# A decoder step on one core: the first loads are cut and spread over two queues, the squares wait for the first conversions, and the first products go to the convolution's banks

## The chip, the cores and the metric

The kernel runs on one core of a Trainium2 chip. It uses the core's five engines: TensorE (PE, matrix products, with PEld for its weight loads), VectorE (DVE), ScalarE (ACT), GpSimd (POOL) and SyncE (SP), which here only issues DMAs. The metric is the device time of one execution in microseconds (us); the median of several runs is compared.

## The reference

One decoder layer is applied to 256 prompt tokens and 8 x 4 sample tokens, 288 columns in all. Cut to what matters here:

```python
h = rmsnorm(x, norm1_g)                              # 2048 channels
proj = einsum("btd,de->bte", h, w_in) + b_in         # 2048 -> 3072
a, gate, z = split(proj, 1024)
u = a * sigmoid(gate)                                # convolution group
c = silu(layernorm(depthwise_causal_conv(concat(hist_conv, u), conv_w, conv_b)))   # 31 taps
d = multiscale_pool(concat(hist_pool, z))            # windows 2, 4, 8, 16
p = einsum("btgc,gce->btge", d, pool_w) * pool_scale
x = x + concat(c, p) @ w_out
h2 = rmsnorm(x, norm2_g)
x = x + square(relu(h2 @ w_ff1)) @ w_ff2             # 2048 -> 8192 -> 2048
y = rmsnorm(x, norm_f)
```

The outputs are `y` for both groups and the last 30 columns of `u` and the last 15 of `z`.

## The kernel before

Channels lie on the 128 partitions and the 288 token columns on the free axis: `xT` holds 16 channel tiles of 288 columns. Weights come from memory in blocks of 1024 input channels by 256 output columns (1 MB, `load`, L146). `split` (L213) turns each block into two halves of four channel tiles, and each half into a high part `whi` (ScalarE, L225) and a low part `wlo`, the rest (VectorE or GpSimd, L228; `SHARE` says how many halves of each kind go to GpSimd). Inputs are split in the same way. `gemm` (L237) forms each result from three products per channel tile: high by high (L250), high weight by low input (L251), low weight by high input (L252).

The input projection is done in 12 groups, in the order of `SEQUENCE`: seven convolution groups, four pool groups, and the eighth convolution group. A convolution group gives 128 columns of `a` (m = 0) and their 128 gates (m = 1). Each group is 16 channel tiles x 2 halves x 3 = 96 products. The text calls the convolution groups blocks 0, 1, 2 and so on. Two blocks of weights belong to each group; the first two, `raw0` and `raw1`, are loaded in quarters, each behind the matching two channel tiles of `xT` (L158, L159).

The norm is applied after the product. `hx` (L271, L272) is `x` times the gain only; the reciprocal root of the mean square is found beside the products: `squares` (L299) squares `xT` on ScalarE (L304) and adds the squares on VectorE (L306), `rsqrt_sums` (L181) adds over the partitions with TensorE (the tile `pt`, L186) and forms the root through a short chain on VectorE and ScalarE to `dg` (L198), and `spread` (L201) brings it to all partitions with one more product (the tile `pr`, L204). ScalarE copies it to `rb` (L395). Before, the program asks for `pt` ahead of channel tile 10 of block 1 and for `pr` ahead of tile 14 of block 1.

`conv_pair` (L320) multiplies a convolution group's result by `rb` (L325), applies the gate (L326, L330), and then runs the 31 taps: the first on ScalarE (L337), 30 on VectorE (L340), the sample tokens on GpSimd and VectorE (L343, L345). The taps stand in a `later` block, which puts them behind all other work in priority. `pool_group` (L354) does the same for a pool group, with its running sums on GpSimd (L369); `dx` is its result split in two parts, `px` the product with `pool_w` (L417, L418).

Results of the products go to banks of PSUM: `acc` has two double banks (the tile `ac`), `cvp` two single banks (tag `cv`, used by the taps' running sum `pc`), `msp` two single banks for the small products.

The order of instructions on each engine isn't the program's. A planner reads the program with its dependencies, plays it through with a model of the costs, and lets each engine take the ready instruction of the highest priority; priority is the program's order, and `later` puts a block behind. On the chip each engine then runs its list in that order. Twelve products of `ones` with itself (L173) run at the start, ahead of the first weights.

Of the kernel before, what the change touches and what calls it, by code (L numbers as in the profile page):

```python
# [9 lines left out]
F32 = mybir.dt.float32  # L10
# [6 lines left out]
P = 128  # L17
# [55 lines left out]
for _k, _n in VEC:  # L73
    OFF[_k] = NV
    NV += _n
CWO = NV
# [4 lines left out]
def trunk_kernel(ctx: ExitStack, tc: tile.TileContext, io):  # L81
# [64 lines left out]
    def load(cuts=((0, 8),), x_cuts=()):  # L146

        raw = wraw.tile([P, 8, 256], F32, name=nm("wr"), tag="wr")
        src = io["w"][next(blocks)]
        for j, (k0, k1) in enumerate(cuts):  # L150
            if j < len(x_cuts):
                a, b = x_cuts[j]
                nc.sync.dma_start(xT[:, a:b, :], io["xT"][:, a:b, :])
            nc.sync.dma_start(raw[:, k0:k1, :], src[:, k0:k1, :])
        return raw

    nc.scalar.dma_start(vec[:, 0:CWO], io["vec"][:, 0:CWO])
# [14 lines left out]
    for j in range(12):  # L172
        nc.tensor.matmul(warm[:, 0:P], ones, ones, start=True, stop=True)  # L173
# [37 lines left out]
    turn = {"n": 0}  # L211

    def split(raw, share=0, cut=4):  # L213
# [3 lines left out]
        for h in range(2):  # L217
# [5 lines left out]
            for k in range(0, 4, cut):  # L223
                src = raw[:, 4 * h + k : 4 * h + k + cut, :]
                nc.scalar.copy(hi[:, k : k + cut, :], src)  # L225
                eng, step = (nc.gpsimd, 2) if slow else (nc.vector, cut)
                for j in range(k, k + cut, step):
                    eng.tensor_tensor(lo[:, j : j + step, :], raw[:, 4 * h + j : 4 * h + j + step, :], hi[:, j : j + step, :].bitcast(F32), op=ALU.subtract)  # L228
            parts.append((hi, lo))

# [45 lines left out]
    def weight_groups():  # L276

        yield [split(raw0, SHARE["first"], 2), split(raw1, SHARE["first"], 2)]
# [20 lines left out]
    def squares():  # L299
# [20 lines left out]
    def conv_pair(i, bk):  # L320
# [4 lines left out]
        nc.vector.tensor_tensor(ag, bk[:, :, :T], both(rb), op=ALU.mult)  # L325
# [28 lines left out]
    def pool_group(g):  # L354
# [236 lines left out]
```

## Time and profile before

| what | us |
|---|---|
| median of 3 runs | 1122.28 (1120.97 to 1122.3) |
| the profiled execution: its own time | 1121.02 |
| its span, first to last instruction | 1119.2 |
| TensorE busy in the span | 1095.0 (98%) |
| VectorE, ScalarE, GpSimd busy | 646.2, 470.1, 185.8 |
| mean granted clock of TensorE | 0.990 |

A row of a timeline gives the start in us from the span's start, the duration, the engine, the line of the kernel, the operation, what it writes and reads, and the shapes; in brackets stands the idle time of the engine just before and what ended it. Products overlap in TensorE's pipeline, so the step from start to start is what counts there; on ScalarE and VectorE too neighbours overlap a little. A row of stages gives, for a stretch of time, each engine's busy time and number of instructions, TensorE's granted clock, the share of the DMA engines' time that is used, and the rate in GB/s.

### The profile page before, as it was taken

How to read it: one execution, taken by the hardware profiler on the slowest of the kernel's cores; microseconds unless marked ns; L12 is line 12 of the kernel's file. 1: busy time of each engine (PE TensorE's matmuls, PEld its weight loads, DVE VectorE, ACT ScalarE, POOL GpSimd, SP SyncE). 2: the span in 40 equal slices, each digit the busy share in tenths (PEclk: the TensorE clock that was granted, in tenths of full speed). 3: DMA queues.
4: the chain of work that ended last, by engine and by line, in shares of the span. 5: the costliest groups of instructions: out<-in, count | busy, mean ns of one | idle time of the engine just before them, and what ended most of it. 6: DMA issues, size and time to landing. Idle time of an engine off the chain costs nothing.

```text
span 1119.2 us, 19178 instructions
## 1 busy us (share of the span) xinstructions
PE 1095.0 (98%) x8220; PEld 1090.7 (97%) x8220; DVE 646.2 (58%) x830; ACT 470.1 (42%) x578; POOL 185.8 (17%) x185
## 2 busy tenths in 40 slices
PE   9999988999999999999999999999999999999995
PEld 8999987999999999999999999999999999999995
DVE  7799999667654444444554444455444445554553
ACT  8444444465444433334443333444433334444441
POOL 1898996512100000000000000000000000000000
PEclk9999998999999999999999999999999999999997
DMA  9545456444444454544445444454544545445432
GB/s 344 186 154 185 151 132 201 154 176 161 160 168 162 161 179 153 179 159 164 175 154 182 153 168 171 155 184 152 172 167 160 180 151 177 162 159 180 152 112 85
DMA packets 31909, 187.00 MB, mean 167 GB/s; under 512 B 3408, under 2 KB 7760, under 8 KB 10448
## 3 DMA queue, kind: packets, MB, share of 16 engines
q1 hardware_dynamic: 31680, 185.73, 48.1%
q8 instruction: 64, 1.05, 0.4%
q14 instruction: 21, 0.17, 0.0%
q10 hardware_dynamic: 144, 0.05, 0.0%
HBM read 181.49 MB, written 4.28 MB: 166 GB/s over the span
## 4 chain that ended last, share of the span: by engine, by line
PE 93%; POOL 2%; DVE 2%; DMA 1%; ACT 1%; issue 1%; SPq 0%; DVEq 0%; ACTq 0%; POOLq 0%
PE ac L250 31%; PE ac L252 31%; PE ac L251 30%; POOL wlo L228 1%; POOL s L369 1%; DMA wr<-in_w 1%; PE pt L186 0%; DMA xT<-in_xT 0%; DVE xT L531 0%; ACT whi L225 0%; ACT hx L271 0%; PE pr L204 0%; DVE px L418 0%; DVE hx L272 0%; DVE pc L340 0%
## 5 line engine op out<-in xcount | busy, mean ns | idle before, releaser
L225 ACT CAST whi<-wr 128x1024 fp32r<-128x1024 f32 (+1 forms) x342 | 355.2, 1040 | 563.6 <-PE ac L251 531.9
L228 DVE TENSOR_TENSOR wlo<-wr,whi 128x1024 fp32r<-128x1024 f32 (+1 forms) x297 | 364.0, 1226 | 352.2 <-ACT whi L225 351.3
L250 PE MATMUL ac<-ax,whi 128*128 128x288 f32 x1024 | 303.4, 296 | 0.0
L250 PE MATMUL ac<-fx,whi 128*128 128x288 f32 x1024 | 303.1, 296 | 0.0
L252 PE MATMUL ac<-ax,wlo 128*128 128x288 f32 x1024 | 301.8, 295 | 0.0
L252 PE MATMUL ac<-fx,wlo 128*128 128x288 f32 x1024 | 301.8, 295 | 0.0
L251 PE MATMUL ac<-ax,whi 128*128 128x288 f32 x1024 | 298.5, 292 | 0.0
L251 PE MATMUL ac<-fx,whi 128*128 128x288 f32 x1024 | 298.5, 292 | 0.0
L251 PEld LDWEIGHTS ac<-ax,whi 128*128 128x128 f32 x1024 | 192.5, 188 | 0.1
L251 PEld LDWEIGHTS ac<-fx,whi 128*128 128x128 f32 x1024 | 192.5, 188 | 0.0
L250 PEld LDWEIGHTS ac<-ax,whi 128*128 128x128 f32 x1024 | 192.4, 188 | 0.1
L250 PEld LDWEIGHTS ac<-fx,whi 128*128 128x128 f32 x1024 | 192.4, 188 | 0.0
L252 PEld LDWEIGHTS ac<-ax,wlo 128*128 128x128 f32 x1024 | 191.5, 187 | 0.0
L252 PEld LDWEIGHTS ac<-fx,wlo 128*128 128x128 f32 x1024 | 191.5, 187 | 0.0
L228 POOL TENSOR_TENSOR wlo<-wr,whi 128x512 fp32r<-128x512 f32 x90 | 119.4, 1358 | 48.1 <-ACT whi L225 48.1
L252 PE MATMUL ac<-hx,wlo 128*128 128x288 f32 x384 | 114.8, 299 | 1.5 <-DVE wlo L228 1.3
L250 PE MATMUL ac<-hx,whi 128*128 128x288 f32 x384 | 114.8, 299 | 0.3 <-ACT whi L225 0.3
L251 PE MATMUL ac<-hx,whi 128*128 128x288 f32 x384 | 112.7, 294 | 0.0
L340 DVE SCALAR_TENSOR_TENSOR pc<-u_all,vec,pc 128x256 f32<-128x256 f32 x232 | 99.4, 480 | 1.2
L252 PEld LDWEIGHTS ac<-hx,wlo 128*128 128x128 f32 x384 | 72.6, 189 | 3.4 <-DVE wlo L228 2.5
L250 PEld LDWEIGHTS ac<-hx,whi 128*128 128x128 f32 x384 | 72.9, 190 | 0.6 <-ACT whi L225 0.5
L251 PEld LDWEIGHTS ac<-hx,whi 128*128 128x128 f32 x384 | 72.9, 190 | 0.1
(109 smaller groups left out, 828.4 us busy)
## 6 DMA issues: line engine op xcount, KB each, us to landing
wr<-in_w SPq DMA_DIRECT2D x167, 1024.0 KB, 4.9
xT<-in_xT SPq DMA_DIRECT2D x8, 288.0 KB, 5.7
wr<-in_w SPq DMA_DIRECT2D x8, 256.0 KB, 5.6
out_u_out<-u_all SPq DMA_DIRECT2D x1, 1208.0 KB, 8.9
out_yT<-xT SPq DMA_DIRECT2D x2, 576.0 KB, 2.9
u_all<-in_hist_c SPq DMA_DIRECT2D x8, 136.0 KB, 6.1
out_z_out<-z_all SPq DMA_DIRECT2D x1, 668.0 KB, 8.1
z_all<-in_hist_p SPq DMA_DIRECT2D x4, 152.0 KB, 5.6
```

What stands on the lines that cost most here:

```text
L225: nc.scalar.copy(hi[:, k : k + cut, :], src)
L228: eng.tensor_tensor(lo[:, j : j + step, :], raw[:, 4 * h + j : 4 * h + j + step, :], hi[:, j : j + step, :].bitcast(F32), op=ALU.subtract)
L250: nc.tensor.matmul(b, wh, xh, start=k == 0, stop=False)
L251: nc.tensor.matmul(b, wh, xl, start=False, stop=False)
L252: nc.tensor.matmul(b, wl, xh, start=False, stop=k == n - 1)
L340: nc.vector.scalar_tensor_tensor(out=dst, in0=up[:, w : w + SEQ], scalar=cwv[:, w : w + 1], in1=pc, op0=ALU.mult, op1=ALU.add)
L369: nc.gpsimd.tensor_tensor(s2[:, m, 2 * w - 1 :], s[:, m, 2 * w - 1 :], s[:, m, w - 1 : ZL - w], op=ALU.add)
```

## The change

It has five parts.

1. The first loads. Only the first 16 columns of `vec` (`norm1_g`, `NG` columns) are loaded ahead, on ScalarE's queue, followed on the same queue by channel tile 0 of the first weight block. SyncE's queue loads tile 0 and then tile 1 of `xT`, tile 1 of the weights, and then two tiles of `xT` and two of the weights in turn, as before. The other columns of `vec` come at the end of these loads. The conversions of the first weight block are cut to match: tiles 0, 1, 2 to 3, and so on.
2. Nine products of `ones` at the start in place of twelve.
3. `squares` begins with a copy on ScalarE of ten elements of the last `whi` tile of block 0 into the first column of the squares' scratch. Each square writes there too, so all eight follow the last conversion of block 0. In the program they stand behind the conversions of block 1, as before.
4. Block 0's products go to two single banks of `cvp` in place of a double bank of `acc`. The sums for the norm (`pt`) are asked for ahead of tile 15 of block 1, and `pr` and the copy to `rb` ahead of tile 3 of block 2; block 2's products stand ahead of `conv_pair(0)` in the program.
5. The multiply by `rb` is done for `a` and for the gates by two instructions of 288 columns each, in all eight convolution groups, in place of one of 576.

```diff
-    def load(cuts=((0, 8),), x_cuts=()):
+    def load():
...
-    nc.scalar.dma_start(vec[:, 0:CWO], io["vec"][:, 0:CWO])
-    raw0 = load(((0, 2), (2, 4), (4, 6), (6, 8)), ((0, 2), (2, 4), (4, 6), (6, 8)))
-    raw1 = load(((0, 2), (2, 4), (4, 6), (6, 8)), ((8, 10), (10, 12), (12, 14), (14, 16)))
-    nc.sync.dma_start(vec[:, CWO:NV], io["vec"][:, CWO:NV])
...
+    def piece(queue, what, a, b):
+        if what == "x":
+            queue.dma_start(xT[:, a:b, :], io["xT"][:, a:b, :])
+        else:
+            queue.dma_start((raw0, raw1)[a // 8][:, a % 8 : a % 8 + b - a, :], firsts[a // 8][:, a % 8 : a % 8 + b - a, :])
+
+    nc.scalar.dma_start(vec[:, 0:NG], io["vec"][:, 0:NG])
+    piece(nc.scalar, "w", 0, 1)
+    piece(nc.sync, "x", 0, 1)
+    piece(nc.sync, "x", 1, 2)
+    piece(nc.sync, "w", 1, 2)
+    for k in range(2, KT, 2):
+        piece(nc.sync, "x", k, k + 2)
+        piece(nc.sync, "w", k, k + 2)
+    nc.sync.dma_start(vec[:, NG:NV], io["vec"][:, NG:NV])
...
-    for j in range(12):
+    for j in range(9):
...
-    def split(raw, share=0, cut=4):
+    def split(raw, share=0, cuts=(0, 4, 4, 8)):
...
+            for a, b in zip(cuts, cuts[1:]):
+                if a // 4 == h and a < b:
+                    nc.scalar.copy(hi[:, a % 4 : a % 4 + b - a, :], raw[:, a:b, :])
+                    eng, step = (nc.gpsimd, 2) if slow else (nc.vector, b - a)
+                    for j in range(a, b, step):
+                        part = slice(j % 4, j % 4 + step)
+                        eng.tensor_tensor(lo[:, part, :], raw[:, j : j + step, :], f32(hi[:, part, :]), op=ALU.subtract)
             parts.append((hi, lo))
+        last_hi.append(hi)
...
-        yield [split(raw0, SHARE["first"], 2), split(raw1, SHARE["first"], 2)]
+        yield [split(raw0, SHARE["first"], (0, 1, 2, 4, 6, 8)), split(raw1, SHARE["first"], (0, 2, 4, 6, 8))]
...
-    def squares():
+    def squares(hi):
+
+        nc.scalar.copy(scratch[:, :, :, 0:1], f32(hi)[:, 3, 0:10].rearrange("p (n k t) -> p n k t", n=5, t=1))
...
-        bk = bank2()
-        gemm(each(bk), hx, **kw)
-        return bk
+        if i:
+            banks = each(bank2())
+        else:
+            banks = [cvp.tile([P, 512], F32, name=nm("ac"), tag="cv") for m in range(2)]
+        gemm(banks, hx, **kw)
+        return banks
...
-        nc.vector.tensor_tensor(ag, bk[:, :, :T], both(rb), op=ALU.mult)
+        for m in range(2):
+            nc.vector.tensor_tensor(ag[:, m, :], banks[m][:, :T], rb, op=ALU.mult)
...
+    last = last_hi[-1]
     first = conv_products(0)
-    squares()
+    squares(last)
     diag = []
-    second = conv_products(
-        1,
-        between={
-            10: lambda: diag.append(rsqrt_sums([t[:, m, :] for t in tot for m in range(2)], 1.0 / D, AF.Sigmoid)),
-            14: lambda: nc.scalar.copy(rb, spread(diag[0])[:, :T]),
-        },
-    )
+    second = conv_products(1, between={15: lambda: diag.append(rsqrt_sums([t[:, m, :] for t in tot for m in range(2)], 1.0 / D, AF.Sigmoid))})
+    third = conv_products(2, between={3: lambda: nc.scalar.copy(rb, spread(diag[0])[:, :T])})
     nc.gpsimd.memset(z_all[:, :, 0:PH], 0.0)
     conv_pair(0, first)
     conv_pair(1, second)
-    for kind, i in SEQUENCE[2:]:
+    conv_pair(2, third)
+    for kind, i in SEQUENCE[3:]:
```

More of the change, by code (lines that the diff above doesn't have):

```diff
@@ L208, in rsqrt_rows @@
         return spread(rsqrt_sums(*args))
-    turn = {"n": 0}
-    def split(raw, share=0, cut=4):
+    turn, last_hi = {"n": 0}, []
+    def split(raw, share=0, cuts=(0, 4, 4, 8)):
         parts = []
@@ L315, in conv_products, with conv_pair @@
         nc.sync.dma_start(u_all[:, i, UO:UL], io["hist_c"][:, i, :])
[L316 to L320 removed]
+        if i:
[4 more added lines that the diff above has]
+        return banks
+    def conv_pair(i, banks):
         up = u_all[:, i, 0:UO]
```

16 lines of the change are left out of this document (4 added, 12 removed).

## The prediction

> **What bounds the kernel now.** I read the page first, then the engines' busy time by stage, then the instructions of the first 40 us on each engine, the landings of the first loads, and last the three long waits of TensorE behind 160 us. Five stages (columns: stretch, length, then busy us and count of PE, PEld, DVE, ACT, POOL, then granted clock, DMA share, GB/s):
>
> ```profile
> 6.30:21.20 14.90, 13.52 (x91) 12.14 (x92) 14.84 (x28) 14.75 (x30) 0.00 (x0) 1.00 1.05 401
> 21.20:37.60 16.40, 16.40 (x132) 16.29 (x131) 7.24 (x13) 8.47 (x12) 10.85 (x9) 1.00 0.90 319
> 37.60:160.00 122.40, 122.24 (x921) 121.67 (x921) 121.74 (x244) 53.63 (x77) 115.85 (x104) 1.00 0.43 150
> 160.00:190.00 30.00, 21.02 (x121) 20.24 (x120) 28.77 (x56) 13.39 (x22) 20.31 (x18) 0.83 0.81 215
> 190.00:1100.00 910.00, 910.00 (x6894) 909.68 (x6893) 465.37 (x474) 375.03 (x433) 37.44 (x33) 1.00 0.47 162
> ```
>
> TensorE sets the end. Its steady step is 910 / 6894 = 0.132 us a product, so 96 of them, one channel block, are 12.67 us. Two places have idle steps: the head, up to 21.2, and 160 to 190 (121 products are 16 us of the 30). In the head ScalarE and VectorE are full (14.75 and 14.84 of 14.90) and so are the DMAs (share 1.05). From 37.6 to 160 TensorE, VectorE (121.74 of 122.40) and GpSimd (115.85) are all full. The change touches the head alone, but it moves the start of VectorE's full stretch too.
>
> The ledger of the head, from TensorE's timeline and VectorE's:
>
> ```profile
> 6.32 0.40 PE L250 MATMUL ac<-hx,whi 128*128 128x288 f32 x1 [0.27 <-ACT whi L225]
> ...
> 21.18 1.78 PE L186 MATMUL pt<-ones,z_all 128*96 128x1 f32 x20
> 22.82 0.38 PE L250 MATMUL ac<-hx,whi 128*128 128x288 f32 x1
> ...
> 35.33 0.65 PE L204 MATMUL pr<-dg,ones 96*128 96x288 f32 x2
> 37.61 0.76 DVE L325 TENSOR_TENSOR ag<-ac,rb 128x576 f32<-128x576 f32 x1 [0.40 <-PE ac L252]
> ```
>
> The second multiply by `rb` waits for the last product of block 1, so block 1 ends at 37.6. Backwards from there: 14.78 us from 22.82, less 0.5 for `pr`, hold 108 products, that is block 1 and the last two channel tiles of block 0. So block 0 ended at about 24.4. From 6.32 to 37.6 are 31.3 us; 192 products (25.3), `pt` (3 columns, 4 parts, 2 passes: 24, about 2.0) and `pr` (0.5) need 27.8. **3.5 us** are lost.
>
> Where: one pair of channel tiles on ScalarE, then on VectorE.
>
> ```profile
> 8.49 0.96 ACT L271 ACTIVATE hx<-xT,vec 128x288 fp32r<-128x288 f32 x2
> 9.36 0.67 ACT L304 ACTIVATE z_all<-xT 128x576 f32<-128x576 f32 x1
> 9.94 0.60 ACT L225 CAST whi<-wr 128x512 fp32r<-128x512 f32 x1
> 10.45 0.96 ACT L271 ACTIVATE hx<-xT,vec 128x288 fp32r<-128x288 f32 x2
> ...
> 9.28 0.94 DVE L272 SCALAR_TENSOR_TENSOR hx<-xT,vec,hx 128x288 fp32r<-128x288 f32 x2
> 10.13 0.75 DVE L306 TENSOR_TENSOR z_all<-z_all 128x576 f32<-128x576 f32 x1
> 10.80 0.69 DVE L228 TENSOR_TENSOR wlo<-wr,whi 128x512 fp32r<-128x512 f32 x1
> 11.40 0.94 DVE L272 SCALAR_TENSOR_TENSOR hx<-xT,vec,hx 128x288 fp32r<-128x288 f32 x2
> ```
>
> By starts a pair costs ScalarE 10.45 - 8.49 = 1.96 us, 0.58 of it the square, and VectorE 11.40 - 9.28 = 2.12, 0.67 of it the sum. TensorE needs 12 x 0.132 = 1.58. So the two converters pace block 0.
>
> **The change, part by part.** *Squares behind the conversions.* The pair loop falls to 1.38 on ScalarE and 1.45 on VectorE, both below TensorE's 1.58. The next bound is the loads. Issue times, with the time to landing of each (the second pair's weights, the eighth's, and the first full load of block 1):
>
> ```profile
> 2.11 0.43 SPq L154 DMA_DIRECT2D wr<-in_w  x1
> ...
> 10.58 0.33 SPq L154 DMA_DIRECT2D wr<-in_w  x1
> ...
> 12.71 0.33 SPq L154 DMA_DIRECT2D wr<-in_w  x1
> ```
> ```profile
> wr<-in_w SPq DMA_DIRECT2D x1, 256.0 KB, 5.6
> ...
> wr<-in_w SPq DMA_DIRECT2D x1, 256.0 KB, 5.5
> ...
> wr<-in_w SPq DMA_DIRECT2D x1, 1024.0 KB, 6.5
> ```
>
> They land at 7.7, 16.1 and 19.2. The same bytes stand ahead of each as before (only 44 KB of `vec` go to the back), and the DMAs are full, so I keep these times. Pair 1: landed 7.7, cast 0.5, low half 0.6, so 8.8; ten of its twelve products follow, 10.1; six more pairs at 1.58 end block 0 at **19.6** (the last pair's weights, 16.1 + 1.1 = 17.2, are early enough). Without `pt` in it block 0 now ends about 3 us sooner than before (24.4 less 1.8).
>
> But block 1 can't start at 19.6. Its first load lands at 19.2. The page's means for half a load:
>
> ```profile
> L225 ACT CAST whi<-wr 128x1024 fp32r<-128x1024 f32 (+1 forms) x342 | 355.2, 1040 | 563.6 <-PE ac L251 531.9
> L228 DVE TENSOR_TENSOR wlo<-wr,whi 128x1024 fp32r<-128x1024 f32 (+1 forms) x297 | 364.0, 1226 | 352.2 <-ACT whi L225 351.3
> ```
>
> So block 1's first cast ends at 20.2 and its third product, the first with a low half, waits for **21.4**; for 22.5 if ScalarE has squares in hand. The last cast of block 0 ends at 16.6, five squares of 0.58 end by 19.7, a sixth by 20.3. The old order didn't meet this wait, for block 0 ended behind it. From 21.4 on 94 products (12.4) and `pt` with its full 2.0, which stands in front of the last channel tile, end block 1 at 35.8, or at 36.9; with `pr` 36.3 to 37.4 against 37.6: **0.2 to 1.3 us won**. I take 1.2, since the casts stand ahead of the squares in the program and so go first once loaded. Most of the 3 us goes to the load.
>
> *Two queues, halved first pieces, nine warm-ups.*
>
> ```profile
> 0.73 0.40 ACTq L157 DMA_DIRECT2D vec<-in_vec  x1
> 0.74 0.38 SPq L153 DMA_DIRECT2D xT<-in_xT  x1
> ...
> 5.64 0.62 ACT L225 CAST whi<-wr 128x512 fp32r<-128x512 f32 x1 [0.27 <-DMA wr<-in_w]
> ```
>
> The first cast follows the landing of a 256 KB piece. A 128 KB piece issued on ScalarE's queue right behind the small `vec`, at 1.13, lands between 4.2 (x0's 3.1 us, landing 3.84) and 5.6; I take 4.8, and the first product at 5.2 in place of 6.32. That buys nothing at the end: channel tiles 0 and 1 are twelve products, done by 7.0, or 7.6 with the worst landing, and pair 1 is not there before 8.1. The cover is the landing at 7.7; if that came 1 us sooner, 1 us of it would count. The extra instructions (one cast and one low half more, about 0.15 us each; one DMA on SP, 0.4, and one on ScalarE's queue) lie in the same shadow. SP's later issues wait for landings, not for SP. The three warm-ups gone are six of 24 passes; the rest end near 4.9, ahead of the first product.
>
> The Trainium skill (Trainium Kernel Development and Optimization, Key Constraints) says that DMAs from several queues run on the same 16 engines, so that a second queue only saves issue time. By it the second queue is worth one issue, 0.4 us; the DMA share of 1.05 here agrees, and the sum has nothing for it.
>
> *`rsqrt` chain later, block 0 in the convolution's banks.* `pt` now stands before channel tile 15 of block 1 and `pr` before tile 3 of block 2. Between them TensorE has 6 + 18 products, 3.2 us. The chain took:
>
> ```profile
> 22.99 0.16 DVE L188 TENSOR_SCALAR st<-pt 96x3 f32<-96x3 f32 x1 [0.30 <-PE pt L186]
> ...
> 25.39 0.77 DVE L198 TENSOR_SCALAR dg<-ident,st 96x96 f32<-96x96 f32 x3
> ...
> 36.45 0.76 DVE L325 TENSOR_TENSOR ag<-ac,rb 128x576 f32<-128x576 f32 x1 [5.61 <-ACT rb L395]
> ```
>
> From the end of `pt` (22.96) to the last `dg` (26.16) 3.2 us: no slack, where there were 9 us. Bounds of the new wait: 0, or 1.2 if a 128x1024 low half stands ahead of `st` on VectorE. I take 0.2. Behind `pr` in TensorE's queue is the rest of block 2. Net **1.0**.
>
> `rb` and so the first multiply come 1.1 us after `pr` (35.33 to 36.45): block 1's end at 35.9, 2.4 for three tiles, the 0.2, 1.1, so **39.6** in place of 36.45. Banks cost TensorE nothing: block 2 needs none of the old ones, and block 3, at 49, comes well behind the multiply.
>
> *The multiply by `rb` cut in two,* for all eight convolution blocks. The nearest row for 288 columns out of a bank:
>
> ```profile
> 172.43 0.51 DVE L418 SCALAR_TENSOR_TENSOR px<-ac,vec,px 128x288 fp32r<-128x288 f32 x1
> ...
> 129.52 3.22 DVE L340 SCALAR_TENSOR_TENSOR pc<-u_all,vec,pc 128x256 f32<-128x256 f32 x8
> ```
>
> Two of 0.51 against one of 0.76 (37.61) are 0.26 more by busy time; neighbours overlap by some 0.08 (a tap is 0.47 alone and 3.22 / 8 = 0.40 in a row), so 0.18, times 8 1.4 us of VectorE; bounds 0.3 (two taps by starts against 0.76) and 2.1. So VectorE's stretch starts 3.2 later and holds 1.4 more: 4.6 us. I cost them at nothing, for what is put off are the taps (0.40 each), which are written to run last, and they have room behind them: the last tap ends by 203.7, and the products that need its outcome start at 239.6:
>
> ```profile
> L340 DVE SCALAR_TENSOR_TENSOR c<-u_all,vec,pc x8: 468/468/481, 73.7 to 203.2; 128x256 f32<-128x256 f32 x8
> ```
> ```profile
> L250 PE MATMUL ac<-mx,whi x128: 294/296/298, 239.6 to 290.0; 128*128 128x288 f32 x128
> ```
>
> Without that cover the price is 4.6.
>
> **Sum.** The profiled execution took 1121.02 (span 1119.2 and 1.8 around it), 1.26 below the median; less 1.0 it is 1120.0. Against the median of the runs that is **1121.3**, the forecast; the bounds above (1.3 won and no wait at `pr`; 0.2 won and the wait of 1.2) give 1121.0 to 1123.3, and with half the 1.3 that the runs shown span, its own range is 1120.3 to 1124.0. This kernel's measurement can't tell less than 0.2%, 2.2 us, from no change.
>
> **The rivals.** All but the last turn on the three waits of 160 to 190:
>
> ```profile
> 166.42 0.61 PE L252 MATMUL ac<-dx,wlo 128*128 128x288 f32 x1 [3.75 <-DVE wlo L228]
> ...
> 174.96 0.40 PE L250 MATMUL ac<-dx,whi 128*128 128x288 f32 x1 [1.26 <-DVE px L418]
> ...
> 182.34 0.40 PE L250 MATMUL ac<-dx,whi 128*128 128x288 f32 x1 [3.97 <-DVE px L418]
> ```
> ```profile
> 167.00:168.00 1.00, 1.00 (x6) 1.00 (x5) 1.00 (x2) 0.00 (x0) 1.00 (x2) 0.50 0.95 385
> ```
>
> *Slower: VectorE's queue sets 160 to 190.* All three waits are for VectorE, full since 36.45. If as many taps stand ahead of these results as now, its 4.6 us arrive whole, whatever the head wins: 1122.3 + 4.6 = 1126.9, or 1124.6 if half is thinned out. For it: the waits' names. Against: the order is written by a planner that puts the taps behind all else, so fewer go first. It decides from the point where VectorE is more than 1.0 us later at the low half of 166.42. Chance 0.19.
>
> *Faster: the waits shrink.* The new order is planned anew over a stretch in which a tap more or less ahead of a result counts 0.40. Five taps fewer before the last wait are 2.0 us, and with a shorter wait the clock needn't drop to half behind it (granted 0.50 at 167, behind the first wait): some 14 products at twice 0.132, 1.8 us. With the head 4.8: 1117.5; with the clock alone or the taps alone about 1119.4. For it: 14 of the 30 us are lost there. Against: the backlog of taps is longer, so there is always one to fill in. Chance 0.33.
>
> The Trainium skill (TensorE: Matmul & The Clock Gate, Part 1) has the half clock follow an idle window of about 3.4 us. The waits of 3.75 and 3.97 bear that out and the 1.26 did not; by it the gap before block 1, 1.8 to 2.9 us, stays free of it.
>
> *The squares don't make way:* all eight go ahead of block 1's first cast, which ends at 22.4; the low half is there at 23.6, block 1 with `pr` ends at 38.5: 0.9 lost, 1123.2, if `pt` still comes late. Chance 0.04.
>
> **The numbers.** Forecast 0.44 (0.36 within, 0.05 faster, 0.03 slower), slower 0.19 (0.01 of it within), faster 0.33, squares 0.04 (within): faster 0.38, same 0.41, slower 0.21. The range 1116.8 to 1125.8 reaches into both sides.
>
> **What would show it.** Right: no square among the first conversions; block 0 done near 19.6; a gap of 1.8 to 2.9 us before block 1 whose releaser is ScalarE or VectorE behind the load of 19.2; first multiply at 39 to 40; waits behind 160 us of 7 to 11 us in all. Wrong: block 1's load landing before 18, `pt` lying in the gap (then 1.7 more is won), a wait of over 1.2 us at `pr`, or the waits behind 160 us changing by more than 2 us.

## The result, and the profile after

| | median us | runs | profiled execution: own time, span | first feed-forward eviction | from there to the end |
|---|---|---|---|---|---|
| before | 1122.29 | 1120.97 to 1122.88 | 1121.02, 1119.2 | 310.78 | 808.4 |
| after | 1131.27 | 1129.83 to 1132.8 | 1132.80, 1131.0 | 329.34 | 801.7 |

The change made the kernel slower: 1.0082 times, with an interval from 1.0064 to 1.0100. The two columns at the right cut the span at the start of the first eviction of the feed-forward part (the tile `t`), behind everything that the change touches. Up to there the changed kernel lost 18.6 us, twice the difference of the medians; behind it, where both run the same instructions, it won 6.7. Both have to be explained.

The rows of the cut, from VectorE's timelines: the first and the last of 32 evictions, before and then after.

```profile
310.78 0.76 DVE L496 SCALAR_TENSOR_TENSOR t<-ac,r 128x576 f32<-128x576 f32 x1 [1.08 <-ACT r L494]
...
1002.93 0.76 DVE L496 SCALAR_TENSOR_TENSOR t<-ac,r 128x576 f32<-128x576 f32 x1 [1.00 <-PE ac L252]
```
```profile
329.34 0.76 DVE L512 SCALAR_TENSOR_TENSOR t<-ac,r 128x576 f32<-128x576 f32 x1 [1.05 <-ACT r L510]
...
1015.67 0.76 DVE L512 SCALAR_TENSOR_TENSOR t<-ac,r 128x576 f32<-128x576 f32 x1 [0.96 <-PE ac L265]
```

They are 692.15 us apart before and 686.33 after, in a stretch in which TensorE never stops: a step of 132.2 ns a product against 131.1.

The stages of the changed kernel, in the columns of the prediction's first fence:

```profile
6.30:21.20 14.90, 13.71 (x94) 12.67 (x93) 12.23 (x24) 13.45 (x28) 0.00 (x0) 1.00 1.03 394
21.20:37.60 16.40, 14.69 (x100) 14.38 (x100) 10.17 (x7) 8.58 (x10) 11.23 (x8) 0.90 0.86 279
37.60:160.00 122.40, 122.40 (x931) 122.29 (x931) 115.37 (x243) 54.70 (x77) 110.11 (x101) 1.00 0.45 159
160.00:190.00 30.00, 14.45 (x82) 13.23 (x81) 29.48 (x50) 11.19 (x18) 22.55 (x22) 0.68 0.66 183
```

Behind them, TensorE alone (its busy time and products, then clock, DMA share and GB/s):

```profile
190.00:240.00 50.00, 44.32 (x300) 0.85 0.32 111
```

ScalarE and VectorE are no longer full in the head, as forecast, but the stage from 21.2 to 37.6 holds 100 products where it held 132. From 160 to 240 TensorE stands still for 15.55 + 5.68 = 21.2 us, where it was 8.98, and its granted clock falls to 0.68 in the last row of the stages (0.83 before). What it waited for in that stretch (us in total, times, longest):

```profile
PE ac L263 <- ACT dx L403: 10.5, 2, 5.6
PE ac L265 <- DVE wlo L240: 7.2, 1, 7.2
PE ac L263 <- DVE ag L344: 1.9, 1, 1.9
```

The head, from TensorE's timeline and then one row of ScalarE's and one of VectorE's (a row without brackets had no idle time before it):

```profile
20.49 0.29 PE L265 MATMUL ac<-hx,wlo 128*128 128x288 f32 x1
21.97 0.50 PE L197 MATMUL pt<-ones,z_all 128*96 128x1 f32 x4 [1.19 <-DVE z_all L321]
22.68 0.40 PE L263 MATMUL ac<-hx,whi 128*128 128x288 f32 x1 [0.21 <-ACT whi L236]
...
23.94 0.44 PE L265 MATMUL ac<-hx,wlo 128*128 128x288 f32 x1 [0.73 <-DVE wlo L240]
24.18 0.44 PE L263 MATMUL ac<-hx,whi 128*128 128x288 f32 x1
...
37.21 1.78 PE L197 MATMUL pt<-ones,z_all 128*96 128x1 f32 x20
43.70 0.65 PE L215 MATMUL pr<-dg,ones 96*128 96x288 f32 x2
```
```profile
21.60 1.98 ACT L236 CAST whi<-wr 128x1024 fp32r<-128x1024 f32 x2
```
```profile
44.82 1.55 DVE L344 TENSOR_TENSOR ag<-ac,rb 128x288 f32<-128x288 f32 x4 [3.88 <-ACT rb L412]
```

Block 0 ends at 20.6, nearly 4 us sooner than before. Then TensorE has two products and four `pt` in 3.3 us, and from 23.94 it steps at 0.24 us, half clock, up to 27.5. Block 1 ends at 39.7 (`pt` ends at 39.0 and six products follow), which with `pr` is 2.6 us later than before. `pr` comes at 43.70, and the first multiply by `rb` at 44.82 in place of 36.45. From 45 to 160 TensorE is busy without a stop, so all of the later loss shows behind 160.

### The profile page after: what moved, and what is told of

It reads as the page before. It is cut to its first block, busy times and chain, and to the rows that moved or that the text cites. A ratio compares the mean times of both kernels' runs of the same rounds, so it can differ in the third digit from the quotient of the medians.

```text
span 1131.0 us, 19188 instructions
## 1 busy us (share of the span) xinstructions
PE 1093.4 (97%) x8214; PEld 1088.2 (96%) x8214; DVE 652.6 (58%) x839; ACT 471.4 (42%) x580; POOL 184.6 (16%) x185
## 4 chain that ended last, share of the span: by engine, by line
PE 93%; DVE 3%; ACT 1%; DMA 1%; issue 0%; SPq 0%; POOL 0%; DVEq 0%; POOLq 0%
PE ac L263 31%; PE ac L264 31%; PE ac L265 30%; DVE pc L359 1%; DMA xT<-in_xT 1%; DMA wr<-in_w 1%; PE pt L197 0%; DVE xT L547 0%; ACT whi L236 0%; ACT hx L284 0%; DVE wlo L240 0%; ACT z_all L319 0%; DVE px L434 0%; PE pr L215 0%; DVE d L396 0%
## 5 line engine op out<-in xcount | busy, mean ns | idle before, releaser
L236 ACT CAST whi<-wr 128x1024 fp32r<-128x1024 f32 (+2 forms) x343 | 355.4, 1037 | 567.3 <-PE ac L264 547.4
L240 DVE TENSOR_TENSOR wlo<-wr,whi 128x1024 fp32r<-128x1024 f32 (+2 forms) x298 | 370.4, 1243 | 350.6 <-ACT whi L236 349.5
L265 PE MATMUL ac<-ax,wlo 128*128 128x288 f32 x1024 | 298.3, 291 | 0.0
L265 PE MATMUL ac<-fx,wlo 128*128 128x288 f32 x1024 | 298.2, 291 | 0.0
L240 POOL TENSOR_TENSOR wlo<-wr,whi 128x512 fp32r<-128x512 f32 x90 | 123.8, 1404 | 54.5 <-ACT whi L236 32.8
```

Source lines behind the costliest of these rows:

```text
L236: nc.scalar.copy(hi[:, a % 4 : a % 4 + b - a, :], raw[:, a:b, :])
L240: eng.tensor_tensor(lo[:, part, :], raw[:, j : j + step, :], f32(hi[:, part, :]), op=ALU.subtract)
L265: nc.tensor.matmul(b, wl, xh, start=False, stop=k == n - 1)
```

## The experiments

Each run is read by five numbers: the start of the first multiply by `rb`, the start of GpSimd's first running sum of the pool groups (`s<-z_all`), the time for which TensorE stands still from 160 to 240, the first feed-forward eviction, and the stretch from there to the end. The programs of *before*, *dummies* and *two, before* are the same up to the eviction, as are *after* and *two, after*: 310.78, 312.68 and 312.99 against 329.34 and 326.22. So one execution tells the eviction to about 3 us, and the loss is 13 to 19, with 15.6 between the means.

| run | what | first multiply | first pool sum | still, 160 to 240 | eviction | rest | median us |
|---|---|---|---|---|---|---|---|
| | before | 36.45 | 119.68 | 9.0 | 310.78 | 808.4 | 1122.3 |
| e4 | loads, cuts, warm-ups alone | 36.52 | 119.76 | 10.4 | 311.86 | 801.6 | 1115.66 |
| e3 | and the squares held back | 41.08 | 121.94 | 10.7 | 316.06 | 808.3 | 1124.14 |
| e5 | and new banks, `pt` and `pr` late | 45.72 | 131.01 | 19.9 | 328.25 | 801.7 | 1127.88 |
| | after: and the cut multiply | 44.82 | 128.16 | 21.2 | 329.34 | 801.7 | 1131.27 |
| e6 | before, cut multiply alone | 36.79 | 120.26 | 9.2 | 311.92 | 801.8 | 1116.69 |
| e8 | before, `pr` at tile 13 | 36.21 | 117.96 | 9.2 | 310.84 | 808.4 | 1120.56 |
| e1 | after, GpSimd held at pool_w | 45.81 | 130.22 | 19.7 | 328.38 | 808.3 | 1136.70 |
| e2 | after, squares behind block 1's casts | 44.84 | 128.24 | 18.6 | 325.85 | 801.7 | 1130.01 |
| e9 | before, first multiply held back | 46.25 | 130.06 | 11.4 | 326.71 | 801.8 | 1129.90 |
| e10 | after, channel sums moved | 45.36 | 125.96 | 19.7 | 325.74 | 801.1 | 1128.89 |
| e11 | after, `pt` and `pr` early | 39.18 | 120.41 | 10.6 | 313.37 | 801.6 | 1125.81 |
| e12 | e4 with the sums of e10 | 36.76 | 119.17 | 9.4 | 310.44 | 808.3 | 1122.28 |

The profiled execution isn't always a middle one: those of e3 (1126.16 us) and e5 (1131.67) lie above the medians of their runs, and that of e11 (1116.79) is the fastest of five.

### A low half shut out by GpSimd (e1)

The longest wait of the changed kernel, 7.2 us for a low half, pointed at one instruction, the first half of the `pool_w` block on VectorE:

```profile
162.43 8.47 DVE L240 TENSOR_TENSOR wlo<-wr,whi 128x1024 fp32r<-128x1024 f32 x1
```

It took 8.47 us while GpSimd ran without a gap to 169.8. The edit makes GpSimd read a column of that half, so that it has to wait for it:

```diff
                         eng.tensor_tensor(lo[:, part, :], raw[:, j : j + step, :], f32(hi[:, part, :]), op=ALU.subtract)
+                    if share == SHARE["pool_w"] and not slow:
+                        nc.gpsimd.tensor_copy(few2, f32(lo[:, part, :])[:, 0, 0:1])
```

> The changed kernel with two tiny GpSimd copies added: each reads one column of a low half of the pool_w block, so that GpSimd, which runs nine instructions back to back from 160.7 to 169.8 us, has to stop in the middle of that run until VectorE has made the half. All else keeps its order but for a few instructions behind 170 us. Theory 1 (the low half, 8.47 us long where others take 1.21, is shut out by GpSimd's run, and TensorE's wait of 7.2 us at 167.4 is its price): the half ends by 168 and not 170.9, the wait falls to 3 to 4.5 us, the time falls to 1126 to 1128.5. Theory 2 (VectorE's queue is simply late, because the first multiply moved from 36.5 to 44.8 us and the multiply is cut): the half is as long or VectorE late elsewhere, the time stays at 1130 to 1132. Theory 3 (any edit gives another plan, and the sum of its waits comes out anywhere): no bound, 1120 to 1133.

VectorE's low half and TensorE's waits:

```profile
164.48 2.34 DVE L240 TENSOR_TENSOR wlo<-wr,whi 128x1024 fp32r<-128x1024 f32 x1
```
```profile
172.13 0.40 PE L265 MATMUL ac<-dx,wlo 128*128 128x288 f32 x1 [2.53 <-DVE wlo L240]
176.06 0.58 PE L263 MATMUL ac<-dx,whi 128*128 128x288 f32 x1 [1.83 <-DVE ag L344]
186.81 0.61 PE L263 MATMUL ac<-dx,whi 128*128 128x288 f32 x1 [7.53 <-ACT dx L403]
```

The half shrank to 2.34 us and the first wait to 2.53, but the waits for `dx` were longer (12.8 us in all, 10.5 in the changed kernel), and the eviction came at 328.38. Theory 1 falls as the cause. The run of *two, after* shows the same by itself: its program has the same order there, the half took 2.33 us without any help, and its eviction stood at 326.22. The shut-out of 8.47 us is an event of one execution, worth some 3 us in it (329.34 against 326.22), and not the loss.

### The parts one by one (e3, e4, e5, e6, e8)

e4 has the new loads, cuts and nine warm-ups on the kernel before; e3 the squares' copy besides; e5 is the changed kernel with the multiply whole for blocks 1 to 7; e6 is the kernel before with the multiply cut; e8 moves one number:

```diff
-            14: lambda: nc.scalar.copy(rb, spread(diag[0])[:, :T]),
+            13: lambda: nc.scalar.copy(rb, spread(diag[0])[:, :T]),
```

> The changed loads, conversions and nine warm-ups alone on the kernel before: the squares stay among block 0's conversions, where ScalarE waits for pieces of the loads. By my forecast's sum block 0 would end 19.6 to 21.5 us with the squares in between costing ScalarE 8 x 0.6 us; if ScalarE is the bound of block 0, its last conversion comes at 20 to 21 and block 0 ends at 23 to 24, as before (24.4), with the load of block 1 landing as before: 1121 to 1123. If the loads are the bound, block 0 ends at 21 to 22, block 1 at 35 to 36.5: 1119.5 to 1121.5. Theory 3: 1120 to 1133 whatever the head does.

> The changed loads, conversions, warm-ups and the place of the squares alone; the row sums at tile 10, the spread at tile 14, block 0's results in the two-bank tile and the multiply in one piece, as before. Theory 1 with the head's loss of 2.5 us at block 1's end: 1124 to 1126 if the pool_w halves do not meet a run of GpSimd, up to 1132 if they do. Theory 2 (the later first multiply and the cut multiply carry the middle's 6 us): the first multiply stands near 40 us and is whole, so about half of the loss is gone, 1126 to 1128. Theory 3: anywhere from 1120 to 1133.

> The changed kernel with the first multiply whole again (576 columns from the two-bank tile) for blocks 1 to 7; block 0 keeps its two single banks and its two multiplies. It is read by the start of the first feed-forward eviction (310.8 us before, 329.3 in the changed kernel, 316.1 with loads, warm-ups and squares alone) and by the stretch from there to the end. Theory 2 (VectorE's queue sets 160 to 190 us, and what is late in it adds up): the cut costs seven times 446 x 2 - 750 ns = 1.0 us of VectorE, the rest is the first multiply's 44.8 against 36.5 us: the eviction starts at 326 to 329. Theory 1 (a low half shut out by GpSimd): by the plan, 320 to 326 if the pool_w halves take 1.2 to 2.4 us, 329 if one takes over 6. The rest of the time goes by TensorE's rhythm behind it, 801.7 or 808.3 us: 1127 to 1137.

> The kernel before with the first multiply in two pieces of 288 columns for every block, nothing else. Theory 2: eight times 0.14 us of VectorE, about 1.1 us, so that the first feed-forward eviction starts at 311.5 to 313 against 310.8 before. Theory 3 (another plan, other waits): 306 to 320. The rest of the time goes by TensorE's rhythm, 801.7 or 808.3 us.

> The kernel before with the spread of the row sums offered at tile 13 of block 1 and not 14, nothing else. Theory 2: the first multiply starts within 0.3 us of its place before (36.5), so the first feed-forward eviction starts within 1 us of 310.8. Theory 3 (another plan, other waits): 306 to 320. Theory 4: behind the eviction either 808.3 or 801.7 us, so 1118 to 1124.

By the eviction, the loads alone lost 1.1 us (inside the spread), the squares held back 4.2 more, the new place of `pt`, `pr` and banks 12.2 more, the cut multiply 1.1, the same 1.1 that it lost alone. Each step is the difference of two single executions. Taking the rest of the table and the 1.8 us around the span off the medians puts the eviction of e3 at 314.0, of e5 at 324.4 and of the changed kernel at 327.8 (estimates). By these each part moves by some 2 us, the cut multiply to 3.4, and the large step stays that of `pt`, `pr` and banks. e6 and e8 reorder VectorE's list in many places and GpSimd's in a few, and leave the eviction at 311.92 and 310.84: two new plans that leave the first multiply in its place don't make the loss (theory 3). It sits in the parts that move the first multiply: to 41.08 with the squares, to 45.72 with `pr` late.

Part of why the squares cost 4.2 can be read in e4's TensorE timeline:

```profile
21.24 1.78 PE L197 MATMUL pt<-ones,z_all 128*96 128x1 f32 x20
22.88 0.38 PE L262 MATMUL ac<-hx,whi 128*128 128x288 f32 x1
```

With the squares among the conversions `pt` is ready when block 0 runs out of work, and fills the time until block 1's first weights are converted. With the squares held back `pt` isn't ready, the time is a gap, and `pt` is paid in full later. In e3 TensorE also stood still for 1.66 us at 41.89, until the first multiply had emptied block 0's double bank for block 2; the changed kernel, with block 0 in the convolution's banks, has no such stop.

### Squares out of the way of block 1 (e2)

```diff
-    last = last_hi[-1]
     first = conv_products(0)
+    last = last_hi[-2]
     squares(last)
```

> The changed kernel with the copy that holds the squares back reading block 1's first converted group in place of block 0's last, so that ScalarE makes block 1's first two conversions before any square. Theory of the head (six squares from 18.1 to 21.6 us stand ahead of the conversions whose load landed at 20.3, the gap they lengthen puts TensorE at half clock from 24.4 to 27.5): the first conversion starts at 20.4, block 1's third product at 22.0 to 23.0 and not 23.9, the half clock is shorter or gone, block 1 ends 1.3 to 3 us earlier, the time is 1128 to 1130 if nothing behind changes. Rival (the gap is set by the load and by the wait for the low half, and the clock drops anyway): block 1 ends less than 0.7 us earlier, 1130.5 to 1131.5. Behind 45 us the order is the same as in the changed kernel, so theory 1 and theory 2 of the middle both leave the waits at 160 to 190 us at their 14 us.

Two rows of ScalarE and of TensorE:

```profile
21.29 1.99 ACT L236 CAST whi<-wr 128x1024 fp32r<-128x1024 f32 x2 [4.01 <-DMA wr<-in_w]
```
```profile
22.39 0.41 PE L263 MATMUL ac<-hx,whi 128*128 128x288 f32 x1 [2.07 <-ACT whi L236]
...
23.65 0.52 PE L265 MATMUL ac<-hx,wlo 128*128 128x288 f32 x1 [0.73 <-DVE wlo L240]
23.97 0.44 PE L263 MATMUL ac<-hx,whi 128*128 128x288 f32 x1
```

ScalarE now stood idle for 4.01 us and its cast was released by the load, at 21.29, against 21.60 with six squares ahead of it. The third product came 0.29 us earlier, half clock followed all the same, and the first multiply stayed at 44.84, as the rival has it. But the load was later as well. Its issue and its time to landing, in the changed kernel and then in e2:

```profile
13.59 0.33 SPq L150 DMA_DIRECT2D wr<-in_w  x1
wr<-in_w SPq DMA_DIRECT2D x1, 1024.0 KB, 6.7
```
```profile
12.99 0.33 SPq L150 DMA_DIRECT2D wr<-in_w  x1
wr<-in_w SPq DMA_DIRECT2D x1, 1024.0 KB, 8.2
```

It landed at 20.3 in the changed kernel and at 21.2 in e2. So the squares held the cast of the changed kernel's profiled execution for 1.3 us behind the landing (20.3 to 21.60), and in e2 a later landing took nearly all of that back. The run doesn't tell load and squares apart.

### The late multiply by itself (e9)

```diff
     nc.gpsimd.memset(z_all[:, :, 0:PH], 0.0)
+    for _ in range(20):
+        nc.vector.tensor_scalar(rb, rb, 1.0, None, op0=ALU.mult)
     conv_pair(0, first)
```

> The kernel before with twenty multiplications of the spread row by 1.0 on VectorE, in place, between the copy that makes it and the first multiply; they only hold VectorE and so the first multiply back. At 0.3 to 0.45 us each they move the first multiply from 36.5 to 43 to 45.5 us, where the changed kernel has it (44.8). Theory 5 (the late first multiply makes VectorE's taps late; GpSimd's in-order queue stands still for the add of the channel sums that waits for a last tap, 108.05 us before and 118.81 in the changed kernel; from there GpSimd runs without a gap, so the sums of the pool groups and TensorE's products behind them are late by all of it): the add starts at 115 to 120 us, the first feed-forward eviction at 320 to 329 against 310.8, though the head is that of before. Rival (the lateness is taken up by the taps, which run last, as the prediction had it): the eviction at 310 to 313. Rival (only another plan): anywhere, 306 to 330, with the add not later than 112.

VectorE's first multiply, and GpSimd's first pool sum:

```profile
46.25 1.42 DVE L325 TENSOR_TENSOR ag<-ac,rb 128x576 f32<-128x576 f32 x2
```
```profile
130.06 1.73 POOL L369 TENSOR_TENSOR s<-z_all 128x422 f32<-128x422 f32 x2
```

On the untouched head of the kernel before, a first multiply 9.8 us later moved the first pool sum by 10.4 us and the eviction by 15.9, or by 14.6 from the mean of before's three. That is as much as the change lost, but it isn't the changed kernel's way of losing it. TensorE's timeline has a stop that the changed kernel lacks:

```profile
47.15 0.58 PE L250 MATMUL ac<-hx,whi 128*128 128x288 f32 x1 [9.57 <-DVE ag L325]
```

The kernel before holds blocks 0 and 1 in the two double banks of `acc`, so block 2 has no bank until the first multiply has read block 0. TensorE waited 9.57 us for it, and everything behind came later together, the pool sums too. From 160 to 240 it stood still for 11.4 us, against 9.0 before and 21.2 in the changed kernel, and it didn't wait for `dx` at all. So e9 shows that a late first multiply is dear in the kernel before; whether the taps take up the lateness when TensorE doesn't wait for the bank, as the prediction had it, this run doesn't test. One detail of theory 5 came out otherwise: the add of the channel sums came at 114.58, just under the forecast, and its own wait was 0.78 us. GpSimd had waited before, for `u_all` itself:

```profile
48.34 5.43 POOL L343 TENSOR_TENSOR prd<-u_all,vec 128x248 f32<-128x248 f32 x8 [7.11 <-DVE u_all L330]
```

### Where the lateness goes on (e10)

GpSimd's rows before, then after; `sum_c` is the add of the channel sums, and the releaser in brackets is the last tap of a block on VectorE:

```profile
108.05 0.81 POOL L349 TENSOR_TENSOR sum_c<-c,c 128x288 f32<-128x288 f32 x1 [2.24 <-DVE c L340]
...
119.68 1.75 POOL L369 TENSOR_TENSOR s<-z_all 128x422 f32<-128x422 f32 x2
...
146.70 1.72 POOL L369 TENSOR_TENSOR s<-s 128x416 f32<-128x416 f32 x2
```
```profile
118.81 0.81 POOL L368 TENSOR_TENSOR sum_c<-c,c 128x288 f32<-128x288 f32 x1 [4.28 <-DVE c L359]
...
128.16 1.73 POOL L388 TENSOR_TENSOR s<-z_all 128x422 f32<-128x422 f32 x2
...
158.20 2.55 POOL L240 TENSOR_TENSOR wlo<-wr,whi 128x512 fp32r<-128x512 f32 x2
160.71 1.72 POOL L388 TENSOR_TENSOR s<-s 128x416 f32<-128x416 f32 x2
```

GpSimd runs its list in order. The add waits for a tap that VectorE makes late, and behind it stand the low halves and all sums of the pool groups. From there GpSimd has no gap up to 168 in either kernel, so a late start stays late: 8.5 us at the first sum. At the last sum of the second group it is 14.0, because between the last sum of the first group and that of the second the new plan has four pairs of low halves where the old had two (5.1 us). Then `dx` is late, and TensorE waits for it (10.5 us in the waits above). VectorE has a share in that: it is full there (29.48 of the 30 us from 160 to 190), and it took up the sums of the third group 7.2 us after GpSimd had ended them (175.45 to 182.60), where before that took 0.6 us (162.84 to 163.46). e10 takes the add's wait away: the first add reads the third pair of blocks, so that no add is asked for before it.

```diff
-            if i % 2 and i > 1:
+            if i in (5, 7):
-                for m in range(2):
-                    nc.gpsimd.tensor_tensor(sum_c[:, m, :], (cs[0] if i == 3 else sum_c)[:, m, :], cs[i // 2][:, m, :], op=ALU.add)
+                for x, m in [(x, m) for x in ((2, 1) if i == 5 else (3,)) for m in range(2)]:
+                    nc.gpsimd.tensor_tensor(sum_c[:, m, :], (cs[0] if x == 2 else sum_c)[:, m, :], cs[x][:, m, :], op=ALU.add)
```

> The changed kernel with the channel sums added in another order: the first add reads the first and the third pair of channel blocks in place of the first and the second, so that no add waits for a last tap before the third pair is done. Theory 5: GpSimd's idle time of 4.28 us before the add at 118.81 is gone, the pool groups' first sum starts at 122 to 125 and not 128.16, the first feed-forward eviction at 322 to 326 against 329.3; if the moved add waits in its new place as long, the gain is lost there and the row shows it. Rival (GpSimd's wait is only a symptom, TensorE waits for VectorE itself): the eviction stays at 328 to 330.

The first sum came at 125.96, 2.2 us earlier and somewhat later than expected (GpSimd now waited 3.13 us for a cast instead), and the eviction at 325.74, inside the forecast. But TensorE stood still from 160 to 240 as long as without the edit (19.7 us, 12.0 of them for `dx`), and three executions with the add in its old place and the same order behind block 1 have the eviction at 329.34, 326.22 and 325.85 (e2). By the medians e10 is 0.8 to 2.4 us shorter than these three. So the add's wait isn't shown to make the loss; whether GpSimd's list or VectorE's makes `dx` late stays open.

### The late `pr` undone, the rest kept (e11)

```diff
-    second = conv_products(1, between={15: lambda: diag.append(...)})
-    third = conv_products(2, between={3: lambda: nc.scalar.copy(rb, spread(diag[0])[:, :T])})
+    second = conv_products(1, between={10: lambda: diag.append(...)})
+    third = conv_products(2, between={0: lambda: nc.scalar.copy(rb, spread(diag[0])[:, :T])})
```

> The changed kernel with the row sums at tile 10 of block 1 in place of 15 and the spread at tile 0 of block 2 in place of 3; banks and multiplies stay changed. Theory 5: the first multiply starts at 41 to 42 us and not at 44.8, the add on GpSimd at 110 to 113, the first feed-forward eviction at 316 to 319, near the 316.1 of the kernel with loads, warm-ups and squares alone. Rival (the changed banks or the order in which blocks are issued makes the middle slow): it stays at 326 to 330.

```profile
39.18 1.55 DVE L344 TENSOR_TENSOR ag<-ac,rb 128x288 f32<-128x288 f32 x4 [3.53 <-ACT rb L412]
```
```profile
120.41 1.73 POOL L388 TENSOR_TENSOR s<-z_all 128x422 f32<-128x422 f32 x2
```

New loads, squares, banks and cut multiply stay, the first multiply comes at 39.18, and the eviction at 313.37, better than forecast: 2.6 us later than before for a multiply 2.7 us later. TensorE stands still for 10.6 us from 160 to 240, and no longer for `dx`. Neither the banks nor the cut make the middle slow.

Two things make this execution look better than the kernel is. It is the fastest of five; if the rest of the others took 801.6 or 808.4 us, their evictions lie at 315 to 317.5 (an estimate), near the forecast and still 8 us or more ahead of any with the changed order. And its head ran at full clock, though up to tile 10 of block 1 it has the instructions of the changed kernel and had the same three waits before block 1's third product (1.19, 0.21 and 0.73 us). TensorE from 24 to 28, in the changed kernel and in e11 (busy time and products, then clock, DMA share and GB/s):

```profile
24.00:28.00 4.00, 4.00 (x19) 0.57 1.04 335
```
```profile
24.00:28.00 4.00, 4.00 (x33) 1.00 1.01 329
```

So about 1.6 of the 5.6 us by which its first multiply came earlier are the clock, and not the place of `pr`.

### TensorE's rhythm (e7, e12, e13, e14)

The stretch behind the eviction came out at 801.1 to 802.0 or at 808.3 to 808.8 in all profiles, never between (e7's 808.5 has its own insertions and both steps in it), and e6's ten runs lie in two groups as far apart: six at 1114.9 to 1117.6, four at 1122.1 to 1124.1. e7 puts one, two, three and four matmuls of one column into the third group of the four feed-forward chunks; e13 and e14 put two into the first chunk alone, of the kernel before and of the changed one:

```diff
-            gemm(each(bk), x1)
+            gemm(each(bk), x1, between={8: dummies} if g == 2 else {})
```

> The kernel before with one, two, three and four matmuls of one column into a bank that nobody reads, in the middle of the third group of the first, second, third and fourth feed-forward chunk. Their own time is about 0.06 us each, 0.6 in all. Theory 4 (TensorE's stream runs at one of two steady rhythms, 132.2 or 131.15 ns a product, falls into one of them at each interruption and keeps it until the next): the pace changes in some of the four chunks from 132.2 to 131.15 and stays so until the next insertion; each chunk at the lower value is 1.6 us shorter, the time 1115 to 1123. Rival (the pace belongs to the build, its addresses or its chip): one pace in all four, 1122.5 to 1123.5.

Neighbouring evictions in the first, second and third chunk of e7, behind the insertion in each:

```profile
344.97 0.76 DVE L496 SCALAR_TENSOR_TENSOR t<-ac,r 128x576 f32<-128x576 f32 x1 [1.00 <-PE ac L252]
357.67 0.76 DVE L496 SCALAR_TENSOR_TENSOR t<-ac,r 128x576 f32<-128x576 f32 x1 [0.99 <-PE ac L252]
...
548.28 0.76 DVE L496 SCALAR_TENSOR_TENSOR t<-ac,r 128x576 f32<-128x576 f32 x1 [0.96 <-PE ac L252]
560.87 0.76 DVE L496 SCALAR_TENSOR_TENSOR t<-ac,r 128x576 f32<-128x576 f32 x1 [0.97 <-PE ac L252]
...
750.37 0.76 DVE L496 SCALAR_TENSOR_TENSOR t<-ac,r 128x576 f32<-128x576 f32 x1 [1.00 <-PE ac L252]
763.07 0.76 DVE L496 SCALAR_TENSOR_TENSOR t<-ac,r 128x576 f32<-128x576 f32 x1 [1.00 <-PE ac L252]
```

A group of 96 products took 12.70 us in the first chunk, 12.59 behind the second insertion, up to the third, and 12.70 again behind that. Within one execution of one program, on unchanged instructions, the stream changed its step at an interruption and kept it until the next. So it comes neither with the build nor with the change alone. Programs do seem to differ in how often they fall into it: before's runs lie together near 1122 (65 of 67, the other two at 1117.9) and its profile has the slower step, the changed kernel's near 1131 with the faster one, and e11's are two at 1116.8 to 1118.6 and three at 1125.8 to 1127.7.

> The kernel before with two matmuls of one column into a bank that nobody reads, in the middle of the third feed-forward group of the first chunk, nothing else. In the run with one, two, three and four of them the stream changed from 132.2 to 131.1 ns behind the two and back behind the three. Theory 4 (the rhythm falls anew at an interruption, by the shift that it gives the stream): the pace is 132.2 before the insertion and 131.1 ns from there to the end, the stretch from the first eviction to the end 802 to 803.5 us and not 808.4, the time 1116 to 1117.5. Rival (the rhythm after an interruption is chance): the runs lie in two groups near 1116 and near 1122.5. Rival (the rhythm belongs to the build): 1122 to 1123.

> The changed kernel with the same two matmuls in the same place. Theory 4: the first eviction stays at 328 to 330 us; the stream, at 131.1 ns before the insertion, may leave that rhythm behind it, as it did behind three of them in the earlier run: 1137 to 1138.5 if it does, 1130 to 1132 if not. The changed kernel's loss against the kernel before at the same rhythm is 15 to 16.5 us either way.

The attempt to set it failed: in e13 the step stayed at 12.69 a group before and behind the insertion (rest 808.8, median 1123.05), in e14 at 12.59 (rest 802.0, median 1129.71). Two insertions don't choose the rhythm; what does stays open.

> The kernel before with the changed loads, conversions and nine warm-ups and with the channel sums in the order of the run before last: the squares, banks, row sums and the multiply stay as before. Theory 5: GpSimd's idle time of 2.2 us before the add at 108 is gone, the first feed-forward eviction starts at 308 to 311 against 311.9 with the loads alone. Rival: the moved add waits as long in its new place, 311 to 313. The rest is 801.7 or 808.3 us by TensorE's rhythm: 1111 to 1122.

(The run that this expectation refers to for the order of the sums is e10.) The eviction came at 310.44 against 311.86 in e4, inside the spread of one execution, and the rest took 808.3. So e4's median of 1115.66, 0.9944 times before (0.9929 to 0.9958) and the lowest of all, is the rhythm: its eviction is no earlier than before's. It beats both kernels, but no run here has an eviction earlier than before's by more than the spread.

## Why the prediction was wrong

The forecast was 1121.3 with a range to 1125.8; the time was 1131.27.

- **Block 0.** Right within a microsecond: it ended at 20.6 (19.6 forecast), and the pair loop fell to 1.37 us. The early first product came at 5.42 (5.2 forecast) and bought nothing there, for TensorE then waited at 8.60 for the next pair's cast.
- **The gap before block 1.** Named and undersized. The load was counted as landing at 19.2, "the same bytes stand ahead"; it was issued 0.9 us later and landed at 20.3. That the casts would go ahead of the squares was wrong: six squares held the first of them until 21.60. The third product came at 23.94 in place of 21.4. The prediction had a later start, 22.5, for squares in hand, but didn't take it.
- **The clock.** The prediction took from the Trainium skill (TensorE: Matmul & The Clock Gate, Part 1) that a gap below about 3.4 us stays free of half clock. In the changed kernel a gap of 3.3 us that was not even empty was followed by 15 products at 0.24 us, 1.6 us too much; in e11 the same gap was not. Together with the third product's 2.5, less 0.3 for the four `pt` done in the gap, this is the head: block 1 ends 3.8 us later than forecast (39.7 for 35.9), and the 1.2 won became 2.6 lost.
- **The place of `pr`.** The wait of 0.2 there didn't come: the row of 43.70 has no idle time before it, and `dg` was done at 40.94. But the planner put `pr` behind five tiles of block 2, not three: 12 products, 1.6 us. With 3.8 from the head, 1.6 and the 0.2 not spent, the first multiply stood at 44.82 and not at 39.6.
- **The step that failed** is "I cost them at nothing, for what is put off are the taps (0.40 each), which are written to run last". The price was TensorE's waits behind 160, which grew by 12.2 us, from 9.0 to 21.2. The cover that the prediction counted on is there, but it has an end. At 39.18, close to the multiply that was forecast, TensorE stood still for 10.6 us in e11, inside the 7 to 11 that the prediction named, and at 41.08, in e3 on the old banks, for 10.7; in all six runs on the new banks with the multiply at 44.7 or later it was 18.6 to 21.2. By these runs the mis-sized first multiply took the kernel past the end of a cover that the prediction took as given. The rival "VectorE's queue sets 160 to 190" had the right place and the wrong size, 4.6 us, since it passed the lateness on one to one. Another path that the prediction left out is GpSimd's list, as good as full in the quoted stage row (115.85 of 122.40): its first pool sum came 8.5 us later. That it makes the waits is not shown (e10).
- **The cut multiply.** Forecast 1.4 us of VectorE; by the profiles the eviction moved by 1.1 with it, twice, which is inside the spread of one execution, and by the medians of e5 and the changed kernel 3.4.
- **The range** rested on the spread of the runs. A rhythm worth 6.7 us wasn't known; it hid that much of the loss of 15.6.

Open: from 41.08 to 44.7 us of the first multiply the eviction moves by some 10 us or more, against about 1 us for each microsecond below. Which list makes `dx` late, the extra pairs of low halves on GpSimd or the taps on VectorE, wasn't measured. No run puts the first multiply late with the new banks and the old head, so the lateness by itself, without the other parts of the change, is not priced.

## What to carry to other kernels

An engine off the critical path that is nearly full can hide a delay only up to a point: before a delay is costed at nothing, work out how much the cover holds, and look for every instruction on another queue that waits for the delayed ones. An experiment that makes the same delay in another kernel may charge for it by another way (here a bank that wasn't free): check where the critical engine stood still before its total is taken as the price. A faster stage only pays up to the next load; work that filled the wait (here `pt`) is worth as much as the time won. Compare kernels at a marker behind the change as well as at the end, since the end may differ for reasons of its own.

## What the runs showed of the hardware

- TensorE's unbroken stream of 288-column products with a new weight each ran at one of two steady steps, 131.1 or 132.2 ns, in every profile behind the first feed-forward eviction; in e7 it changed at an interruption, and over those 800 us it is worth 6.7 us, more than most edits here.
- A subtraction of two SBUF operands on VectorE took 8.47 us in one execution and 2.33 in another of the same order, beside an unbroken run of GpSimd. The Trainium skill (SBUF — State Buffer, Who interferes with whom) says that such an instruction contends with GpSimd's reads and calls the shared port pair an exclusive lock. The half ended 1.1 us after that run of GpSimd did (170.90 and 169.82), and no single instruction of the run was longer than 1.3 us, so VectorE seems to have lost the port several times over; that is inferred and not seen. e1, in which GpSimd has to wait, had the half at 2.34.
- A gap of 3.3 us with four small products and two large ones in it was followed by half rate in the changed kernel, from 23.94 to 27.5, and not in e11, with the same waits in front (granted clock 0.57 and 1.00 from 24 to 28). In the six other profiles with the squares held back half rate followed too. What decides it isn't shown.
